# One 512-column matmul for both input parts in the feed-forward products of a two-layer trunk

## Chip, core and metric

The kernel runs on one core of one Trainium2 chip. The metric is the device time of one execution in microseconds (us). The program is one straight list of instructions for five engines: TensorE (PE, which multiplies, and PEld, its weight loads), VectorE (DVE), ScalarE (ACT), GpSimd (POOL) and SyncE (SP, which issues the large DMAs).

## What is computed

Two token groups of 128 tokens each (a prompt and a sample) pass through two layers with the same weights; 256 tokens stand side by side as columns. Each layer has a mixer sub-layer and a feed-forward sub-layer; the change is about the second:

```
h = RMSNorm(x) * (1 + scale) + shift           # 256 tokens, 2048 features
u = dwconv3(h @ ffn_w_up, ffn_conv) + bias     # 2048 -> 2 x 5632, a width-3 filter over positions
gate, val = split(u, 2)
y = (silu(gate) * val) @ ffn_w_down            # 5632 -> 2048
x = x + g2 * RMSNorm(y)
```

All inputs and outputs are 32-bit floats. `w_mod` (the modulation, which gives shift, scale and g2) is another large weight; its products are spread over the others.

## The kernel before

A product is made from two-part numbers: each 32-bit value is held as `hi` (a cast to the type that TensorE reads in one pass, fp32r) and `lo` (what the cast left over, also fp32r). A product of weight W and input X is the sum of three matmuls into the same 128 x 256 piece of PSUM: W_hi X_hi, W_hi X_lo and W_lo X_hi (`mm3`, lines 335 to 339). Each matmul has a 128 x 128 piece of the weight as its stationary operand and 256 token columns as its moving operand. I call these three a **triple**. Since W_hi is used twice, the weights are loaded into the array three times a triple.

`gemm` (lines 344 to 366) runs over **column groups** of 512 outputs, and in each over the input features in pieces of 512 (`kg`). `weights_` brings in 256 input rows x 512 outputs at a time: one DMA of 512 KB on SP into a `raw` buffer (7 of them), a cast by ACT into a `hi` buffer (line 327), a subtraction by DVE into a `lo` buffer (line 328). There are 3 `hi` and 3 `lo` buffers. I call one such piece of the weight a **step**: 2 row chunks x 4 output blocks of 128 = 8 triples.

In a column group of `gemm` two PSUM banks are open, each with two output blocks. A bank is emptied by `evac` once the last step has passed it. Banks come from a pool of three (`pmm`); a second pool of four (`pg`) serves all else.

The feed-forward part of `layer` (lines 1157 to 1189) has three parts, over 4, 4 and 3 groups of 512 hidden features. Each part first makes, group by group, 512 gate and 512 value columns (the up product: 4 kg, so 8 steps a column group), and `evu` empties a bank with the filter `conv`: per output block one ACT instruction (line 510) and two of DVE (lines 513, 514), which read PSUM. Then come silu, a multiplication and a split into `gh` and `gl`. After that the part's down product adds into the eight tiles `ds`: `evd` copies (part 0), adds (part 1), or calls `fin` (part 2), which adds, squares (ACT), sums the squares on PE into a bank `ss` (line 431) and scales (line 503). `post_norm` uses that sum. Per layer there are 22 up groups of 8 steps and 12 down groups of 8, 8 or 6 steps: 264 steps, 2112 triples; in both layers 528 steps and 4224 triples.

The order on each engine is set by a scheduler at build time, from priorities; `weights` is traced with its priority set 60 instructions ahead (`WP`), so loads and casts stand before the work that surrounds them in the code. The input of the feed-forward, `h`, is made piece by piece in `pre_norm` (lines 485 to 487) while the first column group waits for it.

Of the kernel before, what the change touches and what calls it, by code (L numbers as in the profile page):

```python
# [8 lines left out]
F32 = mybir.dt.float32  # L9
F32R = mybir.dt.float32r  # L10
# [31 lines left out]
# buffers of each pool; columns of the modulation made before the first layer; pieces that GpSimd takes; order of the pieces  # L42
# [7 lines left out]
# how the steps of the scan and of the modulation are spread over the products, by layer and phase  # L50
# [20 lines left out]
class Lazy:  # L71
    """the items of a generator, traced as they are asked for"""
# [10 lines left out]
class Trunk:  # L83
    def __init__(self, ctx, tc, i, o):
# [17 lines left out]
        self.early = 1  # L102
        self.n = 0
# [30 lines left out]
    # ---------------------------------------------------------------- set-up  # L134
# [97 lines left out]
    def modulation(self, l, i):  # L232
        """512 columns of the modulation on the tensor engine: every fourth chunk of the rows in a strip of 32 columns"""
# [58 lines left out]
    # ---------------------------------------------------------------- pieces  # L292
    def split(self, src, nm):
# [5 lines left out]
        return hi, lo  # L299

# [39 lines left out]

    def mm_bank(self, shape=None):
        return self.pmm.tile([128, 2, 256], F32, tag="mm", name=self.name("mm"))

    def gemm(self, wsrc, cols, rhs, kgs, evac, dup={}):
        n = len(kgs)
        for gi, (c0, w) in enumerate(cols):
# [3 lines left out]
            for ki, kg in enumerate(kgs):  # L350
                wt = self.weights(wsrc[512 * kg:512 * kg + 512, c0:c0 + w], 4, w, d)
                for k2 in range(2):
                    hi, lo = wt[k2]
                    xh, xl = (x[k2] if isinstance(x, list) else x[:, 2 * k2:2 * k2 + 2, :] for x in rhs[kg])
                    for m0 in range(0, nm, 2):
                        me = min(m0 + 2, nm)
                        for kk in range(2):
                            for m in range(m0, me):
                                s = slice(128 * m, 128 * m + 128)
                                self.mm3(ps[m0 // 2][:, m - m0, :], hi[:, kk, s], lo[:, kk, s], xh[:, kk, :], xl[:, kk, :],  # L360
# [7 lines left out]
    def gemm_k(self, wsrc, cols, rhs, evac, rates):  # L368
        """like gemm, one group of 512 input features after the other, with all the sums open at once"""
# [4 lines left out]
        for kg in range(4):  # L374
            xh, xl = next(rhs)
            self.rate = rates[kg]
            for gi, (c0, w) in enumerate(cols):
                wt = self.weights(wsrc[512 * kg:512 * kg + 512, c0:c0 + w], 4, w)
                for k2 in range(2):
                    hi, lo = wt[k2]  # L380
                    for j, p in enumerate(banks[gi]):
                        for kk in range(2):
                            for m in range(2):
                                s = slice(256 * j + 128 * m, 256 * j + 128 * m + 128)
                                self.mm3(p[:, m, :], hi[:, kk, s], lo[:, kk, s], xh[:, 2 * k2 + kk, :], xl[:, 2 * k2 + kk, :],
# [36 lines left out]
    def sumsq4(self, ps, src, c0):  # L422
        """like sumsq over 16 chunks, with the sums of every fourth chunk in a strip of 32 columns"""
# [17 lines left out]
    def rsqrt(self, out, src, scale, eps, tmp):  # L441
        """out = 1 / sqrt(scale * src + eps): the table's value, then a Newton step"""
# [14 lines left out]
    def arm(self, after):  # L457
        """brings in the table that the next norm needs, once after is there"""
# [6 lines left out]
    def pre_norm(self, l, which):  # L465
        """a generator: the normed and modulated input, split, by groups of 512 features"""
# [7 lines left out]
        for k in range(4):  # L474
            self.need(l, sh0 // 4 + k, sh0 // 4 + 4 + k)
            hi = self.slab([128, 4, 256], F32R, "hh")
# [150 lines left out]
    def heads(self, l, st, pairs):  # L627
# [4 lines left out]
        for p in pairs:  # L632
# [70 lines left out]
            if p % 2:  # L703
                st["mix"][p // 2] = self.split(at[p // 2], "mx")
# [567 lines left out]
```

## Time and profile before

| | us |
|---|---|
| median of 3 timed executions | 2782.31 |
| lowest and highest of these | 2780.23, 2782.39 |
| span of the profiled execution | 2799.7 |
| PE busy in the span | 2701.2 (96%) |
| PEld busy | 2383.4 (85%) |
| DVE busy | 1695.1 (61%) |
| ACT busy | 1208.4 (43%) |
| mean busy share of the DMA engines on the large queue | 63.5% |

The profiled execution is one run that the hardware recorded; its span, from the first to the last instruction, is 17.4 us more than the median. Matmuls are pipelined: a row shows about 0.28 us for a matmul of 256 columns, but the next one starts much sooner. So the cost of a matmul in a stream is read from start to start, not from its duration, and a busy share of PE near 100% doesn't say how close to its peak it runs.

### The profile page before, as it was taken

How to read it: one execution, taken by the hardware profiler on the slowest of the kernel's cores; microseconds unless marked ns; L12 is line 12 of the kernel's file. 1: busy time of each engine (PE TensorE's matmuls, PEld its weight loads, DVE VectorE, ACT ScalarE, POOL GpSimd, SP SyncE). 2: the span in 40 equal slices, each digit the busy share in tenths (PEclk: the TensorE clock that was granted, in tenths of full speed). 3: DMA queues.
4: the chain of work that ended last, by engine and by line, in shares of the span. 5: the costliest groups of instructions: out<-in, count | busy, mean ns of one | idle time of the engine just before them, and what ended most of it. 6: DMA issues, size and time to landing. Idle time of an engine off the chain costs nothing. (4 is left out here: it accounts for less than half of the span.)

```text
span 2799.7 us, 53893 instructions
## 1 busy us (share of the span) xinstructions
PE 2701.2 (96%) x22531; PEld 2383.4 (85%) x22531; DVE 1695.1 (61%) x2690; ACT 1208.4 (43%) x1747; POOL 124.8 (4%) x130
## 2 busy tenths in 40 slices
PE   7999999989999999999998999999799999999997
PEld 4577778758888988888886987878699999999997
DVE  3377848576564465545556688685766546654665
ACT  2256424344343344334444466353454434443453
POOL 1111000010000000000000020000100000000000
PEclk9999989999999999999999999998899999999998
DMA  9965636778777877788776654443355555555552
GB/s 364 372 208 179 204 102 209 239 249 273 262 260 266 273 265 264 263 268 271 250 256 203 215 184 152 162 141 132 97 181 181 184 185 181 182 183 186 181 181 84
DMA packets 316501, 594.46 MB, mean 212 GB/s; under 512 B 22758, under 2 KB 38146, under 8 KB 316256
## 3 DMA queue, kind: packets, MB, share of 16 engines
q1 hardware_dynamic: 314624, 589.54, 63.5%
q8 instruction: 177, 2.90, 0.4%
q0 software_dynamic: 1632, 1.46, 0.2%
q14 instruction: 68, 0.56, 0.1%
HBM read 583.78 MB, written 7.14 MB: 211 GB/s over the span
## 5 line engine op out<-in xcount | busy, mean ns | idle before, releaser
L328 DVE TENSOR_TENSOR lo<-raw,hi 128x1024 fp32r<-128x1024 f32 (+1 forms) x712 | 854.8, 1204 | 756.0 <-ACT hi L327 716.1
L327 ACT CAST hi<-raw 128x1024 fp32r<-128x1024 f32 (+1 forms) x712 | 733.0, 1030 | 1035.1 <-PE mm L338 839.0
L337 PE MATMUL mm<-hh,hi 128*128 128x256 f32 x3360 | 958.9, 288 | 9.6 <-ACT hh L486 8.7
L338 PE MATMUL mm<-hl,hi 128*128 128x256 f32 x3360 | 953.1, 284 | 1.5 <-DVE hl L487 0.8
L339 PE MATMUL mm<-hh,lo 128*128 128x256 f32 x3360 | 950.7, 284 | 0.9 <-DVE lo L328 0.9
L337 PEld LDWEIGHTS mm<-hh,hi 128*128 128x128 f32 x3360 | 644.4, 192 | 79.4 <-issue 57.9
L338 PEld LDWEIGHTS mm<-hl,hi 128*128 128x128 f32 x3360 | 646.5, 192 | 10.1 <-issue 6.0
L339 PEld LDWEIGHTS mm<-hh,lo 128*128 128x128 f32 x3360 | 645.9, 192 | 5.7 <-issue 3.5
L337 PE MATMUL mm<-gh,hi 128*128 128x256 f32 x1408 | 401.2, 286 | 0.0
L339 PE MATMUL mm<-gh,lo 128*128 128x256 f32 x1408 | 398.8, 283 | 0.0
L338 PE MATMUL mm<-gl,hi 128*128 128x256 f32 x1408 | 398.5, 283 | 0.0
L337 PEld LDWEIGHTS mm<-gh,hi 128*128 128x128 f32 x1408 | 269.6, 192 | 22.8 <-issue 22.6
L339 PEld LDWEIGHTS mm<-gh,lo 128*128 128x128 f32 x1408 | 269.9, 192 | 4.1 <-issue 4.1
L338 PEld LDWEIGHTS mm<-gl,hi 128*128 128x128 f32 x1408 | 270.0, 192 | 3.3 <-issue 3.3
L242 PE MATMUL mb<-raw,cst 128*32 128x512 f32 x1536 | 256.3, 612 | 8.3 <-DMA raw<-in_w_mod 4.3
L510 ACT ACTIVATE u<-mm,vec 128x256 f32<-128x256 f32 x176 | 94.6, 562 | 115.8 <-DVE u L514 84.1
L337 PE MATMUL mm<-mxh,hi 128*128 128x256 f32 x384 | 117.2, 307 | 0.3 <-ACT hi L327 0.3
L338 PE MATMUL mm<-mxl,hi 128*128 128x256 f32 x384 | 112.3, 293 | 0.3 <-DVE mxl L298 0.3
L339 PE MATMUL mm<-mxh,lo 128*128 128x256 f32 x384 | 111.5, 292 | 0.6 <-DVE lo L328 0.6
L513 DVE SCALAR_TENSOR_TENSOR u<-mm,vec,u 128x254 f32<-128x254 f32 x176 | 80.1, 475 | 32.7 <-ACT u L510 32.7
L337 PEld LDWEIGHTS mm<-mxh,hi 128*128 128x128 f32 x384 | 75.3, 197 | 21.0 <-issue 16.6
L496 POOL TENSOR_TENSOR d<-d,rs 128x512 f32<-128x512 f32 x8 | 13.4, 1694 | 1713.0 <-DVE rs L449 1713.0
(344 smaller groups left out, 3130.0 us busy)
## 6 DMA issues: line engine op xcount, KB each, us to landing
raw<-in_w_mod SPq DMA_DIRECT2D x384, 512.0 KB, 5.5
raw<-in_ffn_w_up SPq DMA_DIRECT2D x352, 512.0 KB, 4.5
raw<-in_ffn_w_down SPq DMA_DIRECT2D x176, 512.0 KB, 4.7
raw<-in_w_in SPq DMA_DIRECT2D x80, 512.0 KB, 5.2
raw<-in_w_out SPq DMA_DIRECT2D x64, 512.0 KB, 5.4
raw<-in_w_uq SPq DMA_DIRECT2D x16, 384.0 KB, 4.9
raw<-in_w_in SPq DMA_DIRECT2D x16, 320.0 KB, 3.3
raw<-in_w_in SPq DMA_DIRECT2D x16, 256.0 KB, 3.7
```

What stands on the lines that cost most here:

```text
L242: nc.tensor.matmul(b[32 * q:32 * q + 32, :], self.cst[:, 4 * kg + q, :], r[:, f, :], start=kg == 0, stop=kg == 3)
L327: nc.scalar.copy(hi[:, :, 0:w], r)
L328: nc.vector.tensor_tensor(lo[:, :, 0:w], r, hi[:, :, 0:w], op=ALU.subtract)
L337: mm(out, whi, xhi, start=start, stop=False)
L338: mm(out, whi, xlo, start=False, stop=False)
L339: mm(out, wlo, xhi, start=False, stop=stop)
L496: e.tensor_tensor(d, d, self.bc(rs, 2), op=ALU.mult)
L510: nc.scalar.activation(u[:, m, :], ps[:, m, :], AF.Identity, scale=w1, **kw)
L513: nc.vector.scalar_tensor_tensor(uv[:, :, 1:128], pv[:, :, 0:127], w0, uv[:, :, 1:128], op0=ALU.mult, op1=ALU.add)
```

## The change

Both parts of an input now lie in one tile, `duo`: 128 x 2 (hi, lo) x 2 (feature chunks) x 256 columns. `split2`, `pre_norm` and the end of the scan write such tiles; where there was one ACT cast and one DVE subtraction of 1024 columns there are now two of 512 each. All other products still use three matmuls of 256 columns, through `mm2`, on the new layout.

In the feed-forward a new `gemm_wide` takes the place of `gemm`. An output block has a PSUM bank of its own, and W_hi is loaded once: one matmul of 512 columns sends X_hi and X_lo through it, into the two halves of the bank, then a matmul of 256 columns adds W_lo X_hi to the first half. The halves are added when the bank is emptied. The four banks of a column group come from both pools in turn (3 of 7 from `pmm`, 4 of 7 from `pg`).

In the up product the emptying is now per block: ACT copies the second half to an SBUF tile `us` (3 buffers), DVE adds the first half, and the filter's three instructions read `us` and not PSUM. In the down product part 0 copies the second half by ACT and adds the first by DVE; parts 1 and 2 add both by DVE, in two instructions of 256 columns where there was one of 512 per two blocks.

```diff
+    def duo(self, nm):
+        return self.slab([128, 2, 2, 256], F32R, nm)
+
+    def split2(self, src, nm):
+        nc = self.nc
+        out = []
+        for k in range(0, src.shape[1], 2):
+            t = self.duo(nm)
+            nc.scalar.copy(t[:, 0], src[:, k:k + 2, :])
+            nc.vector.tensor_tensor(t[:, 1], src[:, k:k + 2, :], t[:, 0], op=ALU.subtract)
+            out.append(t)
+        return out
...
+    def wide_bank(self):
+        self.wide += 1
+        pool, tag = ((self.pmm, "mm") if self.wide % 7 in (1, 3, 5) else (self.pg, "g"))
+        return pool.tile([128, 2, 256], F32, tag=tag, name=self.name("wm"))
+
+    def gemm_wide(self, wsrc, cols, rhs, kgs, evac):
+        mm = self.nc.tensor.matmul
+        n = len(kgs)
+        for gi, (c0, w) in enumerate(cols):
+            nm = w // 128
+            ps = [self.wide_bank() for _ in range(nm)]
+            for ki, kg in enumerate(kgs):
+                wt = self.weights(wsrc[512 * kg:512 * kg + 512, c0:c0 + w], 4, w)
+                for k2 in range(2):
+                    hi, lo = wt[k2]
+                    x = rhs[kg][k2]
+                    for m in range(nm):
+                        s = slice(128 * m, 128 * m + 128)
+                        for kk in range(2):
+                            mm(ps[m], hi[:, kk, s], x[:, :, kk, :], start=ki == 0 and k2 == 0 and kk == 0, stop=False)
+                            mm(ps[m][:, 0, :], lo[:, kk, s], x[:, 0, kk, :], start=False, stop=ki == n - 1 and k2 == 1 and kk == 1)
+                        if k2 == 1 and ki == n - 1:
+                            evac(gi, m, ps[m])
+                        if m % 2:
+                            yield
+                    self.tick(0.5)
...
-                def evu(gi, ms, ps):
-                    if ms.start == 0:
+                def evu(gi, m, ps):
+                    if m == 0:
                         us[gi] = self.slab([128, 4, 256], nm="u")
-                    c0 = 44 * gi + 4 * gg + ms.start
-                    self.conv(us[gi][:, ms, :], ps, [self.v(l, "ffn_conv", 88 * j + c0, 2) for j in range(3)], self.v(l, "ffn_conv_b", c0, 2))
+                    c = 44 * gi + 4 * gg + m
+                    t = self.small([128, 1, 256], "us", bufs=3)
+                    nc.scalar.copy(t[:, 0, :], ps[:, 1, :])
+                    nc.vector.tensor_tensor(t[:, 0, :], t[:, 0, :], ps[:, 0, :], op=ALU.add)
+                    self.conv(us[gi][:, m:m + 1, :], t, [self.v(l, "ffn_conv", 88 * j + c, 1) for j in range(3)], self.v(l, "ffn_conv_b", c, 1))
...
-            def evd(gi, ms, ps):
-                k = 2 * gi + ms.start // 2
+            def evd(gi, m, ps):
+                k, e = 2 * gi + m // 2, m % 2
                 if part == 0:
-                    ds[k] = self.half([128, 2, 256], nm="d")
-                    nc.vector.tensor_copy(ds[k], ps)
-                elif part == 1:
-                    nc.vector.tensor_tensor(ds[k], ds[k], ps, op=ALU.add)
+                    if e == 0:
+                        ds[k] = self.half([128, 2, 256], nm="d")
+                    nc.scalar.copy(ds[k][:, e, :], ps[:, 1, :])
                 else:
-                    fin(1)(gi, ms, ps)
+                    nc.vector.tensor_tensor(ds[k][:, e, :], ds[k][:, e, :], ps[:, 1, :], op=ALU.add)
+                nc.vector.tensor_tensor(ds[k][:, e, :], ds[k][:, e, :], ps[:, 0, :], op=ALU.add)
+                if part == 2 and e:
+                    done(1, k)
```

`done` is the old `fin` without its addition: the sum of squares and the scaling.

**First place: PE, inside a step of an up group of the second layer.** In the rows `mm` and `wm` are PSUM tiles, `hh`, `hl` and `hx` are input tiles (hi, lo, and both), `hi` and `lo` are the weight's parts; the size is that of the output. Before:

```order
L337 MATMUL mm_28756<-hh_21459,hi_28880 128x256
L338 MATMUL mm_28756<-hl_21460,hi_28880 128x256
L339 MATMUL mm_28756<-hh_21459,lo_28881 128x256
L337 MATMUL mm_28756<-hh_21459,hi_28880 128x256
L338 MATMUL mm_28756<-hl_21460,hi_28880 128x256
L339 MATMUL mm_28756<-hh_21459,lo_28881 128x256
```

After:

```order
L382 MATMUL wm_25186<-hx_19596,hi_25198 128x512
L383 MATMUL wm_25186<-hx_19596,lo_25199 128x256
L382 MATMUL wm_25186<-hx_19596,hi_25198 128x512
L383 MATMUL wm_25186<-hx_19596,lo_25199 128x256
L382 MATMUL wm_25187<-hx_19596,hi_25198 128x512
L383 MATMUL wm_25187<-hx_19596,lo_25199 128x256
```

Three instructions of 256 columns have become one of 512 and one of 256, and two triples follow each other in one bank before the next bank's turn.

**Second place: DVE, at the end of an up group of the second layer.** The first two `lo` are the next group's steps one and two, the third `lo` its step three; `mm_25716` and `mm_25717` are the banks being emptied (two blocks each). Before:

```order
L328 TENSOR_TENSOR lo_25988<-raw_25985,hi_25987 128x1024
L513 SCALAR_TENSOR_TENSOR u_25946<-mm_25716,vec_20856,u_25946 128x2x127
L514 SCALAR_TENSOR_TENSOR u_25946<-mm_25716,vec_20856,u_25946 128x2x127
L328 TENSOR_TENSOR lo_26042<-raw_26039,hi_26041 128x1024
L513 SCALAR_TENSOR_TENSOR u_25946<-mm_25716,vec_20856,u_25946 128x2x127
L513 SCALAR_TENSOR_TENSOR u_25946<-mm_25717,vec_20856,u_25946 128x2x127
L514 SCALAR_TENSOR_TENSOR u_25946<-mm_25716,vec_20856,u_25946 128x2x127
L514 SCALAR_TENSOR_TENSOR u_25946<-mm_25717,vec_20856,u_25946 128x2x127
L513 SCALAR_TENSOR_TENSOR u_25946<-mm_25717,vec_20856,u_25946 128x2x127
L514 SCALAR_TENSOR_TENSOR u_25946<-mm_25717,vec_20856,u_25946 128x2x127
```

After, with banks `wm_23180` to `wm_23183`, one block each:

```order
L344 TENSOR_TENSOR lo_23406<-raw_23403,hi_23405 128x1024
L1215 TENSOR_TENSOR us_23349<-us_23349,wm_23180 128x256
L1215 TENSOR_TENSOR us_23359<-us_23359,wm_23181 128x256
L1215 TENSOR_TENSOR us_23369<-us_23369,wm_23182 128x256
L562 SCALAR_TENSOR_TENSOR u_23348<-us_23349,vec_19182,u_23348 128x2x127
L562 SCALAR_TENSOR_TENSOR u_23348<-us_23359,vec_19182,u_23348 128x2x127
L563 SCALAR_TENSOR_TENSOR u_23348<-us_23349,vec_19182,u_23348 128x2x127
L563 SCALAR_TENSOR_TENSOR u_23348<-us_23359,vec_19182,u_23348 128x2x127
L344 TENSOR_TENSOR lo_23444<-raw_23441,hi_23443 128x1024
L562 SCALAR_TENSOR_TENSOR u_23348<-us_23369,vec_19182,u_23348 128x2x127
L1215 TENSOR_TENSOR us_23379<-us_23379,wm_23183 128x256
```

Four additions have come in, and seven instructions of the emptying instead of two now stand before the next group's third `lo`.

On ACT at the same place there are, after, the copies of three banks and two filter instructions ahead of the next group's third cast:

```order
L343 CAST hi_23405<-raw_23403 128x1024
L1214 COPY us_23349<-wm_23180 128x256
L1214 COPY us_23359<-wm_23181 128x256
L1214 COPY us_23369<-wm_23182 128x256
L559 ACTIVATE u_23348<-us_23349,vec_19182 128x256
L559 ACTIVATE u_23348<-us_23359,vec_19182 128x256
L343 CAST hi_23443<-raw_23441 128x1024
L559 ACTIVATE u_23348<-us_23369,vec_19182 128x256
L1214 COPY us_23379<-wm_23183 128x256
```

Before, one filter instruction stood there between two casts; the copies are new.

**Third place: PE, where the second output group of the last down part begins.** `ss` gets the sums of squares of the group that has just ended. Before:

```order
L337 MATMUL mm_29215<-gh_27981,hi_29218 128x256
L338 MATMUL mm_29215<-gl_27982,hi_29218 128x256
L431 MATMUL ss_29189<-sq_29191,const 32x256 x2
L431 MATMUL ss_29189<-sq_29209,const 32x256 x2
L339 MATMUL mm_29215<-gh_27981,lo_29219 128x256
```

After:

```order
L382 MATMUL wm_25977<-g_24975,hi_25980 128x512
L383 MATMUL wm_25977<-g_24975,lo_25981 128x256
L382 MATMUL wm_25975<-g_24978,hi_25986 128x512
L383 MATMUL wm_25975<-g_24978,lo_25987 128x256
L382 MATMUL wm_25975<-g_24978,hi_25986 128x512
L480 MATMUL ss_25951<-sq_25952,const 32x256 x2
L382 MATMUL wm_25974<-g_24975,hi_25980 128x512
L383 MATMUL wm_25974<-g_24975,lo_25981 128x256
```

The two sums of squares no longer stand together; the second one follows 18 matmuls later, and the scheduler has taken the group's banks in another order (`wm_25975`, `wm_25977`, then `wm_25974`, `wm_25976`), since `ss` holds one of the seven.

Outside the feed-forward the instructions are the same but for the narrower splits; the order there differs in short stretches on DVE and ACT, and in two places among SP's 1199 DMAs.

## Rows read from the trace of the kernel before

**Rows 1.** The page: PE's busy time; TensorE's granted clock in 40 slices.

```profile
PE 2701.2 (96%) x22531; PEld 2383.4 (85%) x22531; DVE 1695.1 (61%) x2690; ACT 1208.4 (43%) x1747; POOL 124.8 (4%) x130
...
PEclk9999989999999999999999999998899999999998
```

**Rows 2.** Stretches: length, busy us (count) of PE, PEld, DVE, ACT, POOL, clock, DMA.

```profile
610.00:642.00 32.00, 31.60 (x256) 27.04 (x255) 27.80 (x76) 19.05 (x41) 0.00 (x0) 1.00 0.70 237
700.00:1400.00 700.00, 699.07 (x5755) 624.23 (x5754) 363.51 (x435) 273.28 (x300) 0.00 (x0) 1.00 0.79 264
2006.00:2028.00 22.00, 21.19 (x151) 20.78 (x152) 19.78 (x58) 13.36 (x33) 0.00 (x0) 0.86 0.32 98
2030.00:2700.00 670.00, 670.00 (x5577) 669.95 (x5577) 387.85 (x440) 306.68 (x339) 0.00 (x0) 1.00 0.57 183
```

**Rows 3.** The page's groups: operands, count | busy us, mean ns | idle before.

```profile
L337 PE MATMUL mm<-hh,hi 128*128 128x256 f32 x3360 | 958.9, 288 | 9.6 <-ACT hh L486 8.7
...
L337 PE MATMUL mm<-gh,hi 128*128 128x256 f32 x1408 | 401.2, 286 | 0.0
...
L513 DVE SCALAR_TENSOR_TENSOR u<-mm,vec,u 128x254 f32<-128x254 f32 x176 | 80.1, 475 | 32.7 <-ACT u L510 32.7
```

**Rows 4.** Timeline of PE in an up group, second layer: start, us, instruction.

```profile
2300.04 0.28 PE L339 MATMUL mm<-hh,lo 128*128 128x256 f32 x1
2300.16 0.28 PE L337 MATMUL mm<-hh,hi 128*128 128x256 f32 x1
2300.28 0.28 PE L338 MATMUL mm<-hl,hi 128*128 128x256 f32 x1
```

**Rows 5.** PE's timeline in the first layer's attention: 384 and 2 x 128 columns.

```profile
332.60 0.33 PE L337 MATMUL b<-ckh,hi 128*128 128x384 f32 x1
332.77 0.33 PE L338 MATMUL b<-ckl,hi 128*128 128x384 f32 x1
332.95 0.33 PE L339 MATMUL b<-ckh,lo 128*128 128x384 f32 x1
333.12 0.28 PE L661 MATMUL b<-hi,ckh 128*128 128x256 f32 x1
333.24 0.28 PE L662 MATMUL b<-hi,ckl 128*128 128x256 f32 x1
```

**Rows 6.** Timeline of ACT, then DVE, inside a group; idle before in brackets.

```profile
2209.52 1.05 ACT L327 CAST hi<-raw 128x1024 fp32r<-128x1024 f32 x1 [1.83 <-PE mm L338]
2212.40 1.05 ACT L327 CAST hi<-raw 128x1024 fp32r<-128x1024 f32 x1 [1.83 <-PE mm L338]
...
2210.60 1.23 DVE L328 TENSOR_TENSOR lo<-raw,hi 128x1024 fp32r<-128x1024 f32 x1 [1.66 <-ACT hi L327]
2213.48 1.23 DVE L328 TENSOR_TENSOR lo<-raw,hi 128x1024 fp32r<-128x1024 f32 x1 [1.66 <-ACT hi L327]
```

**Rows 7.** Groups by form, DVE then ACT, over the span.

```profile
L1143 DVE TENSOR_TENSOR d<-d,mm 128x512 f32<-128x512 f32 x32 | 21.8, 683 | 18.6 <-PE mm L339 17.9
...
L906 DVE TENSOR_TENSOR rw<-rw,ry 128x256 f32<-128x256 f32 x8 | 3.4, 419 | 6.7 <-ACT rh L899 6.7
...
L899 ACT COPY rh<-ry 128x256 f32<-128x256 f32 x16 | 6.0, 374 | 25.3 <-PE ry L887 15.0 <-PE ry L889 10.3
...
L510 ACT ACTIVATE u<-mm,vec 128x256 f32<-128x256 f32 x176 | 94.6, 562 | 115.8 <-DVE u L514 84.1 <-PE mm L339 31.7
...
L427 ACT ACTIVATE sq<-d 128x512 f32<-128x512 f32 x32 | 19.3, 625 | 31.7 <-DVE d L1143 31.3 <-DVE mod L254 0.4
```

**Rows 8.** Waits in 700 to 1400 us: total us, times, longest us.

```profile
ACT hi L327 <- DMA raw<-in_ffn_w_up: 14.7, 5, 4.1
...
PE mm L337 <- DVE u L514: 0.9, 1, 0.9
```

**Rows 9.** Timeline of PE at the end of the last down group.

```profile
2775.16 0.28 PE L339 MATMUL mm<-gh,lo 128*128 128x256 f32 x1
...
2777.43 0.63 PE L431 MATMUL ss<-sq,const 128*32 128x256 f32 x4 [1.36 <-ACT sq L427]
```

More of the change, by code (lines that the diff above doesn't have):

```diff
@@ L102, in __init__ @@
         self.early = 1
+        self.wide = 0
         self.n = 0
@@ L339, in mm3, with mm2 @@
         mm(out, wlo, xhi, start=False, stop=stop)
+    def mm2(self, out, whi, wlo, x, start, stop):
+        self.mm3(out, whi, wlo, x[:, 0, :], x[:, 1, :], start, stop)
+    def wide_bank(self):
[23 more added lines that the diff above has]
+                    self.tick(0.5)
     def mm_bank(self, shape=None):
@@ L353, in gemm @@
                     hi, lo = wt[k2]
-                    xh, xl = (x[k2] if isinstance(x, list) else x[:, 2 * k2:2 * k2 + 2, :] for x in rhs[kg])
+                    x = rhs[kg][k2]
                     for m0 in range(0, nm, 2):
@@ L374, in gemm_k @@
         for kg in range(4):
-            xh, xl = next(rhs)
+            xs = next(rhs)
             self.rate = rates[kg]
@@ L475, in pre_norm @@
             self.need(l, sh0 // 4 + k, sh0 // 4 + 4 + k)
-            hi = self.slab([128, 4, 256], F32R, "hh")
-            lo = self.slab([128, 4, 256], F32R, "hl")
+            out = [self.duo("hx") for _ in range(2)]
             for e in range(2):
+                hi, lo = out[e][:, 0], out[e][:, 1]
                 h = self.half([128, 2, 256], nm="h")
@@ L563, in fourier @@
             yield
-        st["mix"][2] = self.split(out, "mx")
+        st["mix"][2] = self.split2(out, "mx")
     def rotate(self, x, out, bank=None):
@@ L630, in heads @@
         at = st["at"]
-        ckh, ckl, kr, qh, ql = st["A"]
+        ckh, ckl, kr, qx = st["A"]
         for p in pairs:
@@ L640, in heads @@
                     s = slice(128 * m, 128 * m + 128)
-                    self.mm3(ps[0][:, m, :] if m < 2 else ps[1], hi[:, s], lo[:, s], qh[:, kk, :], ql[:, kk, :], kk == 0 and m % 2 == 0, kk == 3 and m > 0)
+                    self.mm2(ps[0][:, m, :] if m < 2 else ps[1], hi[:, s], lo[:, s], qx[kk // 2][:, :, kk % 2, :], kk == 0 and m % 2 == 0, kk == 3 and m > 0)
             nc.scalar.copy(qn, ps[0])
@@ L1028, in rwkv_solve @@
         tt(y, y, b, op=ALU.mult)
-        hi, lo = (self.half([128, 2, 256], F32R, "mx") for _ in range(2))
-        nc.scalar.copy(hi, y)
-        tt(lo, y, hi, op=ALU.subtract)
-        mix = st["mix"].setdefault(3, ([], []))
-        mix[0].append(hi)
-        mix[1].append(lo)
+        st["mix"].setdefault(3, []).extend(self.split2(y, "mx"))
         yield NW
@@ L1135, in layer, with done @@
         pss = [None]
+        def done(which, k):
+            if k == 0:
+                pss[0] = self.bank([128, 256], "ss")
+            self.sumsq4(pss[0], ds[k], 2 * k)
+            self.scale_out(l, which, k, ds[k])
         def fin(which):
@@ L1139, in ev @@
                 k = 2 * gi + ms.start // 2
-                d = ds[k]
-                if k == 0:
-                    pss[0] = self.bank([128, 256], "ss")
-                nc.vector.tensor_tensor(d, d, ps, op=ALU.add)
-                self.sumsq4(pss[0], d, 2 * k)
-                self.scale_out(l, which, k, d)
+                nc.vector.tensor_tensor(ds[k], ds[k], ps, op=ALU.add)
+                done(which, k)
             return ev
```

22 lines of the change are left out of this document (11 added, 11 removed).

## The prediction

> **What bounds the kernel now.** First the page's busy times: PE is at 96%, DVE at 61%, ACT at 43% [rows 1]. Since PE's rows overlap, that alone doesn't say that PE is the bound, so I looked at stretches. From 2030 to 2700 us, inside the second layer's feed-forward, 5577 matmuls fit in 670 us: one every 120.1 ns, at full granted clock, while DVE is busy for 388 us and ACT for 307 [rows 2]. In the timeline they start exactly 0.12 us apart [rows 4], and they stand so on almost the whole way. The first layer's feed-forward (700 to 1400 us) has the modulation mixed in, but PE is as full there, 699 of 700 us, and DMA is at 0.79 [rows 2]. In these 700 us PE waited once for an emptied bank, 0.9 us; ACT sometimes waited for a weight (5 times, up to 4.1 us) without PE showing it [rows 8]. So in both feed-forwards the matmul stream itself is the path, and what shortens a triple shortens the kernel.
>
> What are these 120 ns? The one place with another width at this type is the attention: three matmuls of 384 columns take from 332.60 to 333.12, 0.173 us each [rows 5]. So 128 columns more cost 53.3 ns, which is one column in a cycle of 2.4 GHz. At that rate 256 columns are 106.7 ns and 384 are 160, and at both widths 13.3 ns come on top. That extra goes with the instruction (and its weight load), not with the columns. Right behind them stand two whose moving operand lies in two separate runs of 128 columns (line 661 and 662, where the weight is the moving side and only its value columns are taken); they start 0.12 us apart as well [rows 5].
>
> **The change, part by part.**
>
> *The matmuls.* A triple was 3 x 120 = 360 ns. Now it is one of 512 columns, 213.3 + 13.3 = 226.7 ns, and one of 256, 120 ns: 346.7 ns. That is 13.3 ns less. A matmul of 512 columns at this type is not in the trace; the bounds are that it keeps two extras (no gain) and that the line through 256 and 384 holds (13.3 ns). I take the line, since two widths lie on it. The 4224 triples (2816 up, 1408 down; the down ones are the 1408 of `gh` [rows 3]) give 56.3 us. A step of eight triples falls from 2.88 us, at which casts now follow each other [rows 6], to 2.77.
>
> *Where that is not the path.* While the first column group of a layer runs, DVE makes `h`: it is busy 27.8 of 32 us and 19.8 of 22 us there [rows 2]. DVE's work in that stretch doesn't change, so I count nothing for these two groups, 64 triples each: 128 x 13.3 ns = 1.7 us less gain.
>
> *Emptying a bank, up product.* Each of 176 blocks brings an ACT copy of 256 columns from PSUM (0.374 us by the nearest row) and a DVE addition of 256 (0.419) [rows 7]; the two filter instructions on DVE (0.475 each, by the first [rows 3]) and the one on ACT (0.562 [rows 7]) stay, now reading SBUF. That the read is cheaper or dearer there is bounded by rows of 256 columns, 0.37 to 0.56. Per group DVE has 8 x 1.23 (`lo` [rows 6]) + 4 x (0.42 + 0.95) = 15.3 us in 22.2; ACT 8 x 1.05 + 4 x (0.37 + 0.56) = 12.1. So it fits; what matters is the order at the group's end. Let T be the end of the last step. PE releases the blocks at T - 2.1, T - 1.4, T - 0.7 and T. ACT copies the first three as they come, and DVE adds them, the third by T + 0.3. DVE's four filter instructions for the first two blocks end by T + 2.2. The third cast of the next group can't start before T, since it needs the `hi` buffer that the last step frees (today casts wait for just that, 1.83 us each [rows 6]); behind two filter instructions on ACT it ends by T + 2.0, and its `lo`, behind DVE's four, by T + 3.4. PE needs it at T + 5.5. The bank for the next group's fourth block is the last group's first, added by T - 1; PE wants it at T + 2.1. So nothing waits, with 2 to 3 us to spare. Cost: nothing; the cover is the three `hi` and `lo` buffers, and if DVE were over 2 us later at each of the 68 column groups, that excess would show in full.
>
> *Emptying, down product.* Parts 0 and 1 have the seven banks and the same slack. In part 2 `ss` holds one, so six are left, and DVE has eight additions of 0.42 a group where two of 0.68 [rows 7] stood; PE's order now splits the two sums of squares. The first sum stands 11 matmuls into the new group (T + 1.9); its square on ACT (0.625 [rows 7]) follows additions that, behind a `lo`, end near T + 1.5, and a cast: T + 2.2. So PE waits about 0.3 us there, and as much for a late bank later. I take 0.5 us at each of three transitions in each layer: 3 us (bounds 0 and 1.5 us each, 0 and 9 us).
>
> *The end of each down product* is exposed. Now the last sum of squares starts 2.0 us after the last matmul ends (2775.44 to 2777.43 [rows 9]), through an addition of 0.68, a square and a scaling between. After, by the order and 0.42 an addition, DVE has behind the last matmul: the rest of an addition, a scaling (0.68), two additions, and the square follows: 2.65 us. 0.65 us more, twice: 1.3 us.
>
> *The rest.* Splits of 1024 columns become two of 512 (ACT 0.62 each for 1.05, DVE 0.68 for 1.23, by the rows for 512 [rows 7]): 0.3 us, beside PE work; the first half comes earlier. DMAs are the same in number and size; the first layer must move them 3% faster, so its DMA share goes from 0.79 [rows 2] to about 0.81, which leaves room. The new order of the mixers moves some DVE work past others; I price that at 0 within 5 us either way.
>
> Sum: 56.3 - 1.7 - 3 - 1.3 = 50.3 us off the profiled execution's 2799.7, so 2749.4. The median of the timed runs is 17.4 us lower; no row says where that lies, and I carry the difference over: 2782.3 - 50.3 = **2732 us**.
>
> **The rivals.**
>
> *The extra goes with the columns, or the two runs cost an extra each.* Then a triple stays 360 ns and only the losses are left: 2782.3 + 4.3 = 2786.6. Against it is the row at 384 (it would be 0.180, not 0.173). For it: 512 is beyond both widths. 0.04.
>
> *Most of the extra stays with the triple* and only the start of one matmul is saved, a fifth of it, 2.7 ns: 4096 x 2.7 = 11 us off, with the losses 2782.3 - 11 + 4.3 = 2776, at the edge of what can be told from no change. Against it, the extra is the same in front of the same and of another weight [rows 4]. 0.02. The Trainium skill ("TensorE: Matmul & The Clock Gate", section "Back-to-back issue gap") speaks for this rival: it gives N/2.4 + 2.5 ns for matmuls back to back at the high clock, so 2.5 ns for one matmul less, though it adds that in a real stream loads and matmuls set the pace together. The trace doesn't agree with the 2.5: it has 13.3 ns over the columns at both widths.
>
> *PE starves at the ends of groups* (the other side). DVE's queue holds five to seven emptying instructions before the `lo` that PE wants next. If these took three times the rows' time, as they might if ACT and DVE wait for each other at every block through the three `us` buffers, seven of 0.45 would add 6.3 us, the `lo` would land at T + 9.7 instead of T + 3.4, and PE would wait 4.2 us at each of 44 up groups: +185 - 50, near 2917. It turns the sign from 50.3 / 44 = 1.1 us a group, that is from 3.2 us of delay in that chain. For it: today ACT already waits for DVE at this place, 84.1 us in all behind line 514 [rows 7]. Against: that wait costs PE 0.9 us in 700. 0.05.
>
> *The load is hidden wholly under the longer matmul*: no extra on 512, or none on the 256 after it: 56 us more off, 2676. At 384 nothing of the kind shows. 0.02.
>
> **How the numbers follow.** My forecast has 0.87, the others as said. Its own ends: gain of 56.3 with no loss and 5 from the mixers, 2721; gain 56.3 - 1.7 - 9 - 1.3, less 5 from the mixers and 0.2 us at each of 44 groups, 30: 2752. These ends hold the 8 in 10. About 0.2% (5.6 us) is what a measurement of this kernel can tell from no change. Faster takes the forecast, the third rival and a part of the rest: 0.91; same 0.04; slower 0.05.
>
> **What would show it.** In the profile after: `wm` matmuls of 512 and 256 columns alternating with starts 0.227 and 0.12 apart (0.24 and 0.12: the first rival); a step every 2.77 us in ACT's casts; 4224 matmuls fewer; PE without gaps at group ends in the up product (gaps over 1 us with a `us` or `lo` behind them: the second rival); gaps of some tenths at `ss`. The two feed-forwards should each be about 25 us shorter and the mixers unchanged. I am wrong if the pair takes 360 ns, or if the mixers moved by more than the feed-forward gained.

## The result, and the profile after

The changed kernel takes 2754.3 us (median of 4, 2749.1 to 2756.6), the kernel before 2782.4 beside it: a ratio of 0.987, with a 95% interval of 0.984 to 0.990. So it is 28 us faster; I had forecast 50 us and 2732, and the measured time lies 2 us outside my range. Yet the two profiled executions differ by 52.6 us. What follows is about these 25 us.

The page of the changed kernel: busy time of the engines, and the granted clock in 40 slices (against [rows 1]).

```profile
PE 2647.5 (96%) x18307; PEld 2133.3 (78%) x18307; DVE 1775.4 (65%) x3008; ACT 1280.6 (47%) x1985; POOL 123.7 (5%) x130
...
PEclk9999999999999999999998999998899999999998
```

There are 4224 matmuls fewer, as forecast, and DVE and ACT have 80 and 72 us more to do, far from being full. By stages (layer-0 mixers, layer-0 feed-forward, layer-1 mixers, layer-1 feed-forward, tail; cut at the first feed-forward matmul and the last `ss` of each layer), the profiled execution of before and that of after; the columns are the length, PE's busy time (instructions), the granted clock, the DMA share and GB/s:

```profile
0.00:609.80 609.80, 566.11 (x4723) 0.97 0.70 238
609.80:1495.60 885.80, 882.92 (x7248) 1.00 0.79 263
1495.60:2005.80 510.20, 474.21 (x4159) 0.94 0.49 158
2005.80:2777.40 771.60, 769.35 (x6364) 1.00 0.55 174
2777.40:2799.70 22.30, 8.57 (x38) 0.63 0.27 96
```

```profile
0.00:601.10 601.10, 559.86 (x4722) 0.99 0.71 241
601.10:1468.00 866.90, 863.14 (x5140) 1.00 0.80 268
1468.00:1980.00 512.00, 473.88 (x4156) 0.94 0.48 157
1980.00:2724.90 744.90, 741.47 (x4254) 1.00 0.56 180
2724.90:2747.10 22.20, 9.12 (x38) 0.53 0.30 95
```

The feed-forwards became 18.9 and 26.7 us shorter, the mixers 8.7 shorter and 1.8 longer. Two things stand out: layer 0 gained 8 us less than layer 1, and the layer-1 mixers run at a mean clock of 0.94 in both.

In the stream itself, layer 1, the triple is what I had worked out. PE's timeline (start, duration, instruction):

```profile
2300.01 0.39 PE L382 MATMUL wm<-hx,hi 128*128 128x512 f32 x1
2300.24 0.27 PE L383 MATMUL wm<-hx,lo 128*128 128x256 f32 x1
2300.35 0.40 PE L382 MATMUL wm<-hx,hi 128*128 128x512 f32 x1
2300.58 0.28 PE L383 MATMUL wm<-hx,lo 128*128 128x256 f32 x1
2300.70 0.39 PE L382 MATMUL wm<-hx,hi 128*128 128x512 f32 x1
```

Starts lie 0.23 and 0.115 us apart; over 500 us it is 346.7 ns a pair (counts below), against 360 for the old triple [rows 4].

### The profile page after: what moved, and what is told of

Read it like the earlier page. It is cut to its first block, busy times and chain, and to the rows that moved or that the text cites. A ratio compares the mean times of both kernels' runs of the same rounds, so it can differ in the third digit from the quotient of the medians.

```text
span 2747.1 us, 46006 instructions
## 1 busy us (share of the span) xinstructions
PE 2647.5 (96%) x18307; PEld 2133.3 (78%) x18307; DVE 1775.4 (65%) x3008; ACT 1280.6 (47%) x1985; POOL 123.7 (5%) x130
## 5 line engine op out<-in xcount | busy, mean ns | idle before, releaser
L382 PE MATMUL wm<-hx,hi 128*128 128x512 f32 x2816 | 994.9, 398 | 8.1 <-DVE hx L536 7.4
L383 PE MATMUL wm<-hx,lo 128*128 128x256 f32 x2816 | 783.1, 279 | 0.0
L382 PEld LDWEIGHTS wm<-hx,hi 128*128 128x128 f32 x2816 | 529.2, 188 | 177.9 <-issue 36.9
L383 PEld LDWEIGHTS wm<-hx,lo 128*128 128x128 f32 x2816 | 531.0, 189 | 3.2 <-issue 2.5
L382 PE MATMUL wm<-g,hi 128*128 128x512 f32 x1408 | 498.8, 398 | 0.0
L383 PE MATMUL wm<-g,lo 128*128 128x256 f32 x1408 | 393.7, 280 | 0.0
L382 PEld LDWEIGHTS wm<-g,hi 128*128 128x128 f32 x1408 | 264.1, 188 | 85.3 <-issue 24.7
L383 PEld LDWEIGHTS wm<-g,lo 128*128 128x128 f32 x1408 | 265.2, 188 | 7.2 <-issue 7.1
L353 PE MATMUL mm<-hx,hi 128*128 128x256 f32 x544 | 157.6, 293 | 4.2 <-ACT hx L535 4.2
L354 PE MATMUL mm<-hx,hi 128*128 128x256 f32 x544 | 155.6, 287 | 0.5
L353 PE MATMUL mm<-mx,hi 128*128 128x256 f32 x512 | 155.0, 304 | 0.0
L354 PE MATMUL mm<-mx,hi 128*128 128x256 f32 x512 | 148.6, 291 | 0.0
## 6 DMA issues: line engine op xcount, KB each, us to landing
raw<-in_w_mod SPq DMA_DIRECT2D x384, 512.0 KB, 5.4
raw<-in_ffn_w_up SPq DMA_DIRECT2D x352, 512.0 KB, 4.5
raw<-in_ffn_w_down SPq DMA_DIRECT2D x176, 512.0 KB, 4.3
raw<-in_w_in SPq DMA_DIRECT2D x80, 512.0 KB, 5.1
raw<-in_w_out SPq DMA_DIRECT2D x64, 512.0 KB, 5.1
```

The source lines that it names most:

```text
L353: mm(out, whi, xhi, start=start, stop=False)
L354: mm(out, whi, xlo, start=False, stop=False)
L382: mm(ps[m], hi[:, kk, s], x[:, :, kk, :], start=ki == 0 and k2 == 0 and kk == 0, stop=False)
L383: mm(ps[m][:, 0, :], lo[:, kk, s], x[:, 0, kk, :], start=False, stop=ki == n - 1 and k2 == 1 and kk == 1)
```

## The experiments

**1. A second look at both kernels, and each half of the change alone.** The first and the fourth run repeat the kernels before and after unchanged. The second takes the wide feed-forward alone, with the old layout in the mixers:

```diff
+            if which:
+                out = [self.duo("hx") for _ in range(2)]
+            else:
                 hi = self.slab([128, 4, 256], F32R, "hh")
                 lo = self.slab([128, 4, 256], F32R, "hl")
...
-                self.finish(self.gemm(i["ffn_w_up"][l], [(512 * gg, 512), (DFF + 512 * gg, 512)], h, range(4), evu))
+                self.finish(self.gemm_wide(i["ffn_w_up"][l], [(512 * gg, 512), (DFF + 512 * gg, 512)], h, range(4), evu))
```

The third is the changed kernel with the feed-forward put back to triples, so only the layout is left:

```diff
-                self.finish(self.gemm_wide(i["ffn_w_up"][l], [(512 * gg, 512), (DFF + 512 * gg, 512)], h, range(4), evu))
+                self.finish(self.gemm(i["ffn_w_up"][l], [(512 * gg, 512), (DFF + 512 * gg, 512)], h, range(4), evu))
```

> The kernel before, unchanged, for a second profiled execution. The two traces so far differ by 52.6 us (2799.7 and 2747.1 us of span), the timed runs by 28. Theory A (the missing 22 us lie in the mixers): the first trace of before was long in its layer-0 mixers; a second one has about 2780 us of span, its mixers take about 590 + 505 us (610 + 510 in the first), its feed-forward stages 886 and 772 us as in the first. Theory B (they lie in the feed-forward): the mixers are again 610 + 510 us and the feed-forward stages are together some 20 us shorter than in the first trace. Time 2782 +- 3 by both.

> The kernel before with only the feed-forward's wide matmuls (512 columns, a bank per 128 outputs, the halves added on emptying); the mixers, their splits and their order stay as they were. Theory A (the new layout costs the mixers some 20 us): about 2732 us, 50 below before. Theory B (the feed-forward gives 28 us, the mixers nothing): about 2754 us, as the whole change.

> The changed kernel with the feed-forward put back to three 256-column matmuls for each product and the old emptying: what is left of the change is the layout of the two parts side by side and the mixers' splits and matmuls that follow from it. Theory A: about 2802 us, 20 above before. Theory B: 2782 +- 4 us, as before.

> The changed kernel again beside the others on one chip. Both theories: 2754 +- 4 us; a second trace tells how its stages scatter (the first: 601 + 867 + 512 + 745 us and 22 at the end). Theory A: its mixers are longer in a slower execution. Theory B: its feed-forward stages are.

Measured: before 2782.8; wide alone 2750.8 (0.985 [0.982, 0.988]); layout alone 2801.8 (1.005 [1.002, 1.007]); the whole change again 2753.1. So the layout alone costs 18 us, nearly as theory A said; but the wide feed-forward alone gives 33 us and not 50, nearly as B said. Neither is whole. The stages of the traces (us; the ends of before and after are those shown above):

| | mixers 0 | feed-forward 0 | mixers 1 | feed-forward 1 | tail |
|---|---|---|---|---|---|
| before, first trace | 609.8 | 885.8 | 510.2 | 771.6 | 22.3 |
| before, second trace | 603.8 | 885.9 | 496.6 | 771.5 | 22.0 |
| after, first trace | 601.1 | 866.9 | 512.0 | 744.9 | 22.2 |
| after, second trace | 606.5 | 867.1 | 512.5 | 757.7 | 22.9 |
| wide only | 605.0 | 868.6 | 496.8 | 757.3 | 21.9 |
| layout only | 603.2 | 886.1 | 516.3 | 771.7 | 21.9 |

Two quantities jump. The layer-1 mixers take 497 us or 510 to 516, and the layer-1 feed-forward of a wide kernel takes 745 or 757. The two traces of before, of one and the same program, differ by 19.9 us, and all but 0.3 of it lies in the mixers: 13.6 in layer 1 and 6.0 in layer 0.

*The mixers* first. The 15 us of layer 1 lie in one place, the second block solve of the scan there (small matmuls of 32x32 weights, `px` and `pr`). A stretch of 20 us in it, columns as above: first the first trace of before, then its second, then after.

```profile
1901.00:1921.00 20.00, 20.00 (x143) 0.50 0.14 48
```

```profile
1895.00:1915.00 20.00, 20.00 (x257) 1.00 0.18 53
```

```profile
1878.00:1898.00 20.00, 20.00 (x151) 0.50 0.03 9
```

The granted clock is 0.50 there (1.2 GHz) or 1.00 (2.4), and with it 143 to 151 instructions fit or 257; wide only has 1.00, layout only 0.50. Where it falls, it falls 1 to 4 us behind the first `px` and stays so for 20 to 31 us (41 in one kernel with work added). I call this **the fall**. It can be read without a trace too, from the mean clock of an execution: of the 14 traces of this study the nine with 0.976 to 0.981 have it, and the five with 0.985 to 0.987 don't. By that, with the line drawn at 0.983 (no trace lies between 0.981 and 0.985), 17 of 74 executions of before have the fall, 0 of 6 of wide only, 10 of 12 of layout only, and all 10 of after. The trace that the prediction rests on has it as well, with a mean clock of 0.979, and that is most of its 17.4 us over the median.

The 6 us in the layer-0 mixers are of the same kind. At the first block solve of layer 0 the clock was low for much longer in the first trace of before than in its second, and fewer instructions fit:

```profile
363.00:379.00 16.00, 15.22 (x114) 0.51 0.14 45
```

```profile
363.00:379.00 16.00, 15.23 (x167) 0.89 0.29 83
```

*The feed-forward.* PE's `wm` matmuls of 512 columns in 500 us of layer 1 (busy time and count of PE, then of PEld), in the first and then in the second trace of after:

```profile
2100.00:2600.00 500.00, 500.00 (x1444) 270.43 (x1443) 1.00 0.59 190
```

```profile
2100.00:2600.00 500.00, 500.00 (x1416) 265.89 (x1415) 1.00 0.62 186
```

500 us by 1444 (those at the edges counted in) is 346.3 ns, and by 1416 is 353.1 (wide only has 1417); from the starts in the timelines the two values are 346.7 and 353.3, with nothing between, at the same full clock and with the same instructions. A stretch keeps the value that it has after an interruption. In layer 1 there is none for over 640 us, so almost the whole stage has one; in layer 0 the modulation interrupts every few us, and both occur in one trace. PE in the first trace of after, two uninterrupted stretches, each by its first and last 512-column matmul (39 and 15 of them):

```profile
682.78 0.40 PE L382 MATMUL wm<-hx,hi 128*128 128x512 f32 x1
...
695.95 0.40 PE L382 MATMUL wm<-hx,hi 128*128 128x512 f32 x1
...
743.80 0.39 PE L382 MATMUL wm<-hx,hi 128*128 128x512 f32 x1
...
748.75 0.40 PE L382 MATMUL wm<-hx,hi 128*128 128x512 f32 x1
```

13.17 us over 38 intervals is 346.6 ns; 4.95 over 14 is 353.6. So the triple gains 13.3 or 6.7 ns. Over 2112 triples that is 28 or 14 us a layer: layer 1 measured 26.7 or 14, layer 0 with its mixture 17 to 19.

**2. What makes the fall?** In the new layout PE waits longer at the block solve, for the last transposition of the inverse (`M`). PE's first `px` in wide only, then in after (in brackets the idle time before it and who ended it):

```profile
1874.64 0.74 PE L1042 MATMUL px<-rh,M 32*32 32x64 f32 x10 [0.50 <-DVE M L1022]
```

```profile
1874.07 1.30 PE L1038 MATMUL px<-rh,M 32*32 32x64 f32 x20 [0.78 <-DVE M L1018]
```

I took that wait for the cause (theory A in what follows). One run was to lengthen it in the old mixers, the other to shorten it in the new ones:

```diff
+        if l == 1 and z == 1:
+            nc.vector.tensor_copy(X[:, 24:32, :], X[:, 24:32, :])
         XT = M
         nc.vector.transpose(XT.rearrange("p n t -> p t n"), X)
```

```diff
-                st["mix"][p // 2] = self.split2(at[p // 2], "mx")
+                st["mix"][p // 2] = self.split2(at[p // 2], "mx", nc.gpsimd if l == 1 and p == 3 else None)
```

> The kernel with the wide feed-forward and the old mixers, with one VectorE copy more (128x256, in place, 0.33 us) ahead of the last transposition of the scan's inverse in layer 1; VectorE then also does one weight subtraction (1.14 us) ahead of that transposition, and TensorE has seven more 256-column matmuls (0.84 us) to do before the block solve. TensorE's wait at the block solve should grow from 0.50 us to about 1.1. Theory A (a longer wait there is what sends the clock to half for the 30 us of the block solve, as in the changed kernel): the granted clock is 0.5 there in most executions, the layer-1 mixers take 511 to 516 us and the time is 2754 to 2766 us. Rival (the drop comes from something else of the new layout): the mixers stay at 497 to 498 us and the time at 2740 to 2752.

> The changed kernel with two VectorE subtractions (the low parts of the last attention output in layer 1, 0.69 us each) given to GpSimd; they stand shortly ahead of the last transposition of the scan's inverse there, on which TensorE waits 0.78 us. Theory A: the transposition comes earlier against TensorE's other work, the wait shrinks, the clock stays at full, the layer-1 mixers take 497 us instead of 512 and the time is 2738 us (2751 where the triples run at 353 ns). Rival: the clock falls as before, 2752 us.

Neither did to the wait what it should: it was 0.43 us in the first (no fall, 0 of 5; 2748.6 us) and 1.41 in the second (the fall in 6 of 6; 2765.2). So both agree with the theory and neither tests it. The next pair did. In the changed kernel the transposition was written in the shorter form, with every engine's order untouched; in the old mixers it was made twice.

```diff
-        nc.vector.transpose(XT.rearrange("p n t -> p t n"), X)
+        flat = l == 1 and z == 1
+        nc.vector.transpose(XT if flat else XT.rearrange("p n t -> p t n"), X)
...
-                    mm(px[js, n, :], XT[js, 8 * d + n, :], R[js, n, :], start=n == 0, stop=n == 7, tile_position=(32 * j, 32 * j))
+                    mm(px[js, n, :], XT[js, :, 8 * d + n] if flat else XT[js, 8 * d + n, :], R[js, n, :], start=n == 0, stop=n == 7, tile_position=(32 * j, 32 * j))
```

```diff
         nc.vector.transpose(XT.rearrange("p n t -> p t n"), X)
+        if l == 1 and z == 1:
+            nc.vector.transpose(XT.rearrange("p n t -> p t n"), X)
```

> The changed kernel with one instruction in another form and every engine's order untouched: the last transposition of the scan's inverse in layer 1 writes its rows one after the other (as the first transposition of that tile, 1.25 us) and not 32 elements apart (2.02 us); the block solve loads its weights with that stride instead. TensorE's wait at the block solve, 0.78 us in the changed kernel, should be gone or under 0.1 us. Theory A (that wait sends the clock to half there): the clock stays at full, the layer-1 mixers take 497 us, 15 less, the time is 2738 us (2751 with triples at 353 ns). Rival (the drop hangs on what stands before, the 1.75 us wait for the modulation for one): the mixers stay at 511 to 514 us, the time at 2751 to 2753.

> The wide feed-forward with the old mixers, and that same transposition (2.02 us) made twice, so that the block solve of layer 1 starts later; VectorE then does one weight subtraction (1.14 us) more ahead of it and TensorE fifteen more 256-column matmuls (1.8 us), so its wait of 0.50 us should grow to some 1.5 to 1.9 us. Theory A: the clock falls to half in most executions, the layer-1 mixers take 511 us or more, the time is 2754 (2766 with triples at 353 ns). Rival: 497 to 500 us and 2740 to 2753, as without it.

The first `px`, and then a later stretch, of the kernel with the short transposition:

```profile
1881.64 1.97 PE L1039 MATMUL px<-rh,M 32*32 32x64 f32 x31
```

```profile
1886.00:1906.00 20.00, 20.00 (x149) 0.50 0.06 13
```

And of the one with two transpositions:

```profile
1874.14 1.24 PE L1044 MATMUL px<-rh,M 32*32 32x64 f32 x19 [1.13 <-DVE M L1024]
```

```profile
1878.00:1898.00 20.00, 20.00 (x150) 0.50 0.11 37
```

With the wait gone the clock falls all the same (6 of 6 executions, mixers 509 us, 2760.7 us, 0.990 [0.987, 0.992]). Theory A is dead: the wait is not needed. With a longer wait in the old mixers the clock falls as well (6 of 6, 510 us, 2754.1), so the new layout isn't needed either.

The two traces of before say the same without any edit. Their first `px` (first trace, then second) comes after the same wait, all waits of PE over 0.15 us in the 80 us ahead of it agree within 0.02 us, and yet the clock falls in one of them only:

```profile
1897.38 0.80 PE L989 MATMUL px<-rh,M 32*32 32x64 f32 x11 [0.50 <-DVE M L969]
```

```profile
1891.18 0.80 PE L989 MATMUL px<-rh,M 32*32 32x64 f32 x11 [0.50 <-DVE M L969]
```

The rival in the expectation for the short transposition names one more wait, 1.75 us for the modulation. It stands some 42 us ahead of the block solve in every trace of the new layout and in none of the old one, where the clock falls without it (first trace of before, two transpositions). So that wait isn't needed either.

A last idea was that the small matmuls themselves do it, standing alone. Two runs put full-width matmuls among them, extra work whose result is not used:

```diff
+                wf = l == 1 and z == 1 and j == 0
+                fb = self.bank([128, 256], "fb") if wf else None
                 for n in range(8):
...
+                    if wf and n % 4 == 3:
+                        mm(fb, self.c(C_ONE, 128), X.rearrange("p a b -> p (a b)")[:, 0:256], start=n == 3, stop=n == 7)
```

The second leaves out the condition on `j`.

> The changed kernel with work added, whose result is not used: four full-width matmuls (128x128 weights, 256 columns, fp32, at most some 0.5 us each) among the first sixteen 32x32 matmuls of the block solve in layer 1, one behind every four. The clock fell 1 to 4 us behind the start of these in every trace where it fell. Theory D (it falls because these small matmuls stand alone, whatever wait is ahead of them): with the wide ones among them it stays at full, the layer-1 mixers take about 499 us, the time is 2740 us (2753 with triples at 353 ns). Rival (it falls by what lies earlier, or falls some us later all the same): 512 us and more for these mixers, 2752 to 2756 us.

> As the run before, with such matmuls behind every four of the 32x32 ones in all four steps of that block solve (16 in all, at most 8 us of TensorE's time, part of it in its waits there). Theory D: the clock stays at full, the layer-1 mixers take 500 to 505 us, the time is 2741 to 2746 us (13 more with triples at 353 ns), and if the four of the run before only put the fall off, it is gone here. Rival: 513 to 520 us, 2754 to 2762 us.

Measured 2765.6 and 2780.1 us. By the clock, 5 of 6 and 12 of 12 executions have the fall (the traced one of the first is the sixth; the second's mixers take 528.5 us). So theory D falls too. The sixth execution has the new layout, the wait for `M` and the one for the modulation (1.74 us), and still keeps its clock in the block solve:

```profile
1881.01 0.63 PE L1040 MATMUL px<-rh,M 32*32 32x64 f32 x8 [0.77 <-DVE M L1018]
```

```profile
1885.00:1905.00 20.00, 20.00 (x248) 1.00 0.20 63
```

Its mixers take 505.8 us all the same, in part for two short falls earlier in them (6.8 us each at 0.50, from 1695 and 1791 us).

What stays open is which feature of the work ahead decides. What is shown: in layer 1 the long fall is at one place, costs some 10 to 16 us (more where short falls elsewhere add), has two outcomes for one program, and small shifts of the work around that place turn a program from almost never to almost always. The Trainium skill ("TensorE: Matmul & The Clock Gate", section "What's actually happening") says that the gate's watch on PE's activity runs on its own and doesn't start with the kernel; that would let one program meet it at different points, but no run here tests that.

**3. The two values of the triple.** If the 6.7 ns come at the change between a 512-column and a 256-column matmul, fewer changes should take them away. On wide only, each half step does its eight wide matmuls first, then the eight narrow ones (the last half step of a group four and four, so that banks come free as before):

```diff
-                        for kk in range(2):
-                            mm(ps[m], hi[:, kk, s], x[:, :, kk, :], start=ki == 0 and k2 == 0 and kk == 0, stop=False)
-                            mm(ps[m][:, 0, :], lo[:, kk, s], x[:, 0, kk, :], start=False, stop=ki == n - 1 and k2 == 1 and kk == 1)
+                        for m in ms:
+                            for kk in range(2):
+                                mm(ps[m], hi[:, kk, 128 * m:128 * m + 128], x[:, :, kk, :], start=ki == 0 and k2 == 0 and kk == 0, stop=False)
+                        for m in ms:
+                            for kk in range(2):
+                                mm(ps[m][:, 0, :], lo[:, kk, 128 * m:128 * m + 128], x[:, 0, kk, :], start=False, stop=last and kk == 1)
```

> The wide feed-forward with the old mixers, and the matmuls of each half step in another order: the eight 512-column ones one after the other, then the eight 256-column ones (in the last half step of a column group four and four). Theory C (a 512-column matmul costs 226.7 ns and a 256-column one 120, and the 6.7 ns more of some triples come from the change between the two widths, in a state that a stretch takes up at its start): every stretch runs at 346.7 ns a triple or within 1 ns, the feed-forward stages are 858 and 745 us, the time 2730 +- 3 in every execution. Rival (the state is one of the whole engine, whatever the order): stretches at 353 ns remain, layer 1 is at 745 or 757, the time 2739 or 2752.

Measured: **2735.0 us** (2734.1 to 2739.6; 0.982 [0.979, 0.985]), the fastest kernel here: ahead of after, and 4 us ahead of the two better executions of wide only (2739.3 and 2739.5). Its stages are 603.6, 860.9, 496.5, 749.1 and 22.0. PE in layer 1:

```profile
2302.05 1.12 PE L386 MATMUL wm<-hx,lo 128*128 128x256 f32 x8
2303.00 2.00 PE L381 MATMUL wm<-hx,hi 128*128 128x512 f32 x8
2304.84 1.12 PE L386 MATMUL wm<-hx,lo 128*128 128x256 f32 x8
```

2302.05 to 2304.84 is 2.79 us for eight triples, 349.2 ns each: not the 346.7 that I expected, and the loss is not one per change (eight triples lose 20 ns at two changes). But it is the same in layer 1's whole stretch, and the four executions lie within 5.5 us, so the theory fits the scatter, not the price. That the change of widths is what makes the two values is not shown by it.

The grouped kernel with all four transpositions in the short form:

```diff
-        nc.vector.transpose(XT.rearrange("p n t -> p t n"), X)
+        nc.vector.transpose(XT, X)
...
-                    mm(px[js, n, :], XT[js, 8 * d + n, :], R[js, n, :], start=n == 0, stop=n == 7, tile_position=(32 * j, 32 * j))
+                    mm(px[js, n, :], XT[js, :, 8 * d + n], R[js, n, :], start=n == 0, stop=n == 7, tile_position=(32 * j, 32 * j))
```

> The wide feed-forward with the old mixers and the grouped order of the matmuls, with all four of those transpositions in the shorter form. By both theories the four waits at the block solves (0.5 to 1 us each) shrink: 2732 +- 3 us, 2 to 4 below the grouped kernel. Theory A also has no execution left in which the clock falls in the layer-1 mixers.

Measured 2750.3 us (2736.3 to 2755.1): 15 us slower, since 5 of 6 executions now have the fall (mixers 506.7 us in the trace), though no wait stands ahead of the first `px`. Its sixth is at 2736.3.

## Why the prediction was right, and where it was wrong

Span times mean clock, taken from each execution's own two numbers, puts it together. It leaves out what was lost to a lower clock (a bookkeeping figure: not all of a slow stretch waits for TensorE). Before: 2736 to 2746 us in all 74 executions. After: 2692 to 2697 in 9 of 10, 2711 in one. The rest, span times (1 - clock): before 33 to 42 us in most, up to 62 in those with the fall; after 52 to 61. So by this figure the change gains 48 us (I said 50.3), and against a usual execution of before it pays about 19 back to the clock. That is the 28, within about a microsecond. The stages say the same: against the second trace of before, which has no fall, the first trace of after is 45.6 us shorter in the feed-forwards, 2.7 shorter in the layer-0 mixers and 15.4 longer in the layer-1 mixers.

- **What bounds the kernel**: right. In layer 1 the triple's 28.1 us, less the losses at the two ends, are the 26.7 that its stage gained.
- **The triple, 346.7 ns**: right as one of two values, 346.7 and 353.3. Two widths [rows 5] gave the line, but a stream that alternates widths wasn't in the trace. By the span times clock nine of the ten executions of after have the better value in layer 1; layer 0, interrupted by the modulation, has a mixture. So of the 56.3 us some 48 came (the 45.6 of the two stages and what was lost at their two ends): all of layer 1's 28 and 20 in layer 0, where in that trace some 1200 of 2112 triples run at 353.3. The term was 8 us too large.
- **First column group, -1.7**: of that size. In layer 1 that group takes 27.5 us before and after; PE waits there for `hx` from DVE, 1.6 us in all.
- **Emptying, up product, 0**: right, and by its own schedule. In 700 to 1400 us no wait of PE's is listed. ACT, then DVE, at the end of a column group:

```profile
2162.24 0.37 ACT L1214 COPY us<-wm 128x256 f32<-128x256 f32 x1 [0.32 <-PE wm L383]
```

```profile
2162.27 1.08 DVE L1215 TENSOR_TENSOR us<-us,wm 128x256 f32<-128x256 f32 x3
2163.35 0.98 DVE L562 SCALAR_TENSOR_TENSOR u<-us,vec,u 128x254 f32<-128x254 f32 x2
2164.24 0.87 DVE L563 SCALAR_TENSOR_TENSOR u<-us,vec,u 128x254 f32<-128x254 f32 x2
2165.03 1.22 DVE L344 TENSOR_TENSOR lo<-raw,hi 128x1024 fp32r<-128x1024 f32 x1
```

The third block's copy starts when PE is through with it, 2162.24, so the step ends (T) a block, 0.69 us, later, at 2162.9. The first three additions, four filter instructions, then `lo`, which lands at 2166.2: T + 3.3, where I had T + 3.4. The copies and additions take 0.366 and 0.415 us (0.374 and 0.42 estimated), the filter from SBUF 0.597 on ACT (0.562 from PSUM, and a little over my bound of 0.56) and 0.480 on DVE (0.475): nothing is cheaper there.
- **Transitions in part 2, -3**: too much. No gap over 0.25 us is there in layer 1 between the first column group and the last sums.
- **End of the down product, -1.3**: nearly. PE in after:

```profile
2722.14 0.28 PE L383 MATMUL wm<-g,lo 128*128 128x256 f32 x1
2722.72 0.63 PE L480 MATMUL ss<-sq,const 128*32 128x256 f32 x4 [0.30 <-ACT sq L476]
2724.86 0.41 PE L480 MATMUL ss<-sq,const 128*32 128x256 f32 x2 [1.51 <-ACT sq L476]
```

From the last matmul's end (2722.42) to the last sum 2.44 us; I had 2.65, and 2.0 before [rows 9].
- **DMA, 0.81**: 0.82 in 700 to 1400 us; PE waited for no weight.
- **"The new order of the mixers ... I price that at 0 within 5 us"**: wrong, and this is the step that failed. The layout brings the fall in the layer-1 mixers into all ten executions, 15 us (512 for 497), where about one in four had it.
- **"No row says where that lies, and I carry the difference over"**: wrong too, and the same thing. A row did say it: the clock of [rows 1] has an 8 in its sixth and its twenty-eighth slice (350 to 420 us and 1890 to 1960). The second trace of before has a 9 in both:

```profile
PEclk9999999999999999999999999999899999999998
```

With the fall left in, the sum for the profiled execution, 2749.4, is within 3 us of the same sort of execution of after (a span of 2747.1), and within 5 of the median. That it is so near is in part luck: the feed-forwards gave 4.7 us less than the sum, and the mixers 7 us more, most of it the long fall in layer 0, which that trace of before had and this one of after has not.
- **The rivals**: one matmul less gave 13.3 ns, or 6.7, so neither the first rival's 0 nor the second's 2.7 came; the hidden load didn't either, and PE didn't starve. The 2.5 ns that would go by the Trainium skill ("TensorE: Matmul & The Clock Gate", section "Back-to-back issue gap") don't agree with either value. None of my rivals was about the clock.

## What to carry to other kernels

Before a difference between a profiled execution and the timed ones is carried over, look for stretches of it at a lower granted clock: they may be one of two outcomes of the same program, and a change that only reorders work nearby can fix the worse one in place. Multiply the span by the mean clock to see what an edit does apart from that. Where a stream alternates matmuls of two widths, grouping them by width is worth a try: here the four executions then lay within 5.5 us, while the fall can still come in (the last run).

## What I had not expected of the hardware

- A stream of 512- and 256-column fp32r matmuls has two steady rates, 346.7 and 353.3 ns a pair, at the same clock; it keeps one until it is interrupted. Eight and eight give 349.2.
- The clock can fall to 0.50 for 20 us and more with no wait of PE right ahead of it, while PE shows as busy all the time; one program can do it in some executions and not in others, with the same waits.
- The transposition of 128 x 1024 on DVE takes 1.25 us when its rows are written one after the other and 2.02 when they go 32 elements apart (the same instruction in the kernel with the short form and in after).
